# An encoder on one core: the first chunk gets an engine order of its own, its projections leave PSUM in one multiplication by the norm, and key copies, sink copies and two output weights get places at the end of a chunk

## The chip, the cores and the metric

The kernel runs on one core of one Trainium2 chip. A core has five engines that run side by side, each with its own in-order instruction queue: TensorE (PE, matrix products and transposes, results in the accumulators of PSUM), VectorE (DVE) and ScalarE (ACT) for elementwise work, GpSimd (POOL), and SyncE (SP), which here only issues DMA transfers. POOL issues some of the transfers too. Engines wait for each other through semaphores. The metric is the device time of one execution in microseconds; lower is better.

## What is computed

The reference is a two-layer encoder trunk over two independent sequences, one of 2048 and one of 512 positions, each position with 1024 channels. Layer 0 is windowed attention with grouped keys, learned sinks and a position bias; layer 1 mixes by a Fourier transform. Cut to what matters here:

```python
def attention_layer(x, g, w_in, w_out, sink, rel_bias):
    h = rmsnorm(x, g)
    z = h @ w_in                     # 16 query heads of 64, 4 key heads, 4 value heads, a gate
    q, k, v, gate = ...
    o = banded_gqa_with_sink(q, k, v, rel_bias, sink)   # keys at most 128 positions away
    return x + (o * jax.nn.silu(gate)) @ w_out

def fourier_layer(x, g, w_gate, w_out):
    h = rmsnorm(x, g)
    f = real part of the 2-D DFT of h over (positions, channels of a group), 4 groups
    return x + (f * jax.nn.silu(h @ w_gate)) @ w_out

y = rmsnorm(fourier_layer(attention_layer(x)), final_norm)   # for x_prompt and x_sample
```

In the banded attention a block of 128 queries sees the key block before it, its own and the one after it. The first and the last block of a sequence see only two. The denominator of the softmax also has the exponential of the sink.

## The kernel before

**Precision.** All products are fp32 to nearly full precision: each operand is split into a high part (a rounding copy, made by ACT) and a low part (operand minus high part, made by DVE or POOL), and a product is three matmuls: high by high, high by low, low by high (`matmul3`, line 128). A weight tile is therefore `[128, 2, 1024]`, 1 MB, made from a 512 KB fp32 tile.

**Chunks.** The attention layer runs over five chunks of 512 positions (`CHUNKS`, line 42). The first chunk, `c == 0`, is the whole short sequence; chunks 1 to 4 are the long one. In chunk 0 the weights come as fp32 (`fetch_w`, line 135, a DMA on SP), are split on the chip (`load_w`, line 144: ACT the high part, POOL the low part in four pieces), and are stored to DRAM (`wsd`, a DMA on POOL's queue). Chunks 1 to 4 load the split form from there with one DMA on SP. Split weights share four buffers (tag `w`). The fp32 tiles lie in buffers of the tags `uT` (8) and `x` (4), which other tiles use as well. Two weights of the keys (`LATE`, line 33) are split a second time in the middle of chunk 0, only to be stored; their tile takes a `w` buffer until the store has landed.

**Norms.** The norm's gain is folded into `h`. In chunks 1 to 4 the factor 1/rms is multiplied into `h` as well. In chunk 0 it isn't known early enough, so the products of `h` in raw scale are multiplied by it afterwards: `scaled` (line 366) multiplies a projection in PSUM in place (L369, DVE).

**Heads and the loop.** Eight pairs of heads `p` each need a query projection and a gate projection, in the order of the list `heads` (line 996): 16 projections, each a `Product` of 8 steps `k`, written alternately into the two PSUM banks `pj[0]` and `pj[1]`. The loop over `n` (line 1046) is a software pipeline of 19 iterations: iteration `n` works on half a pair of heads (two blocks of 128 queries) per stage of the pipeline, and PE fills the time between with the next two projections. Its order is written by hand in `PERIOD` (line 36): a list of (step, how many iterations back). Each engine's steps are chained (`seq`, line 178, and `pe`, line 184), so an engine issues them in the order of the list. Instructions that are not chained are placed by the framework's planner, which knows only their data dependences, modelled times and order in the program.

The steps, by engine:

- PE: `A` and `B` are the two projection stretches, 24 matmuls each on half the rows of the array (`beside`, line 483); in iteration `n`, `A` begins the projection `n + 2` in the bank from which projection `n` must have gone. `S1`, `S2` are the scores of two blocks (L582), `T0`, `T1` the transposes of the softmax (L641), `AV1`, `AV2` the products with the values (L682).
- DVE: `b1a` to `b2b` add bias and find the maximum (L601), `r1`, `r2` invert denominators (L615), `m1a`, `m2a`, `m2b` divide (L624, in chunk 0 L628), `lo0`, `lo1` make the low part of the transposed softmax (L658), `add` sums the values (L712), `qL` is the second operation of a projection's exit (L529 or L538).
- ACT: `e1a` to `e2b` are the exponentials (L609), `m1b` a division (L622), `hi0`, `hi1` the high parts (L654), `t2` a copy of the values (L702), `sp` the high part of the gated output (L723), `qH` the first operation of a projection's exit (L527 for a query, L536 for a gate).
- POOL: `mul` multiplies by the gate (L718), `lop` makes the low part (L727).
- `extra0`, `extra1` carry work for the next chunk or the next layer.

A projection leaves its bank through `evac_q` or `evac_g` (lines 524 and 533): in chunk 0 the multiplication L369, then ACT, then DVE, all three reading the bank.

At the head of an iteration stand, unchained, the load of the bias rows of a coming pair (`start`, line 548, a DMA on SP: `b<-rowd`) and `loads[n + 4]()` (line 1056), the weight of the projection four places on: in chunk 0 fetch, ACT's split, POOL's split and store. The sinks (`sinks`, line 560, L562) are copied into the two ends of a pair's bias tile by ACT; for the first pair of a chunk (`p == 0`) the copy is not chained.

**Between chunks.** `out_proj` (line 770) multiplies the gated outputs by the output weights in two halves of columns. The first half's products begin in the last iterations; `rest` (line 830) ends them with 48 matmuls; `evac(0)` loads the residual and adds it; then `mm(1, k)` runs the second half, 96 matmuls, and asks for a weight tile (`load(1, m)`) at every second `k`. For all but the last chunk these steps run at the beginning of the next chunk, together with `make_h` (line 249: DMA `xk`, POOL L263, ACT L267, DVE L268) and `kv_proj` (line 374), which makes keys and values and copies the last 256 key columns of the chunk before to the front (L381, DVE, not chained).

After the five chunks `fourier_phase` (line 1088) does layer 1; the change does not touch it.

Of the kernel before, what the change touches and what calls it, by code (L numbers as in the profile page):

```python
# [40 lines left out]
)  # L41
# [8 lines left out]
def encoder(  # L50
# [93 lines left out]
    def load_w(c, n, name, lo_engine=None, late=None, w32=None):  # L144

        w = wp.tile([P, 2, D], F32R, align_bytes=LINE, tag="w", bufs=4, name=f"w{name}")
        if c == 1 and n in AGAIN:
            w32 = xtile([P, D], F32, f"w32{name}")
            SP.dma_start(w32, w_in[n])
            ACT.copy(w[:, 0], w32)  # L150
            DVE.tensor_tensor(w[:, 1], w32, f32(w[:, 0]), ALU.subtract)
            POOL.dma_start(f32(wsd[n]), f32(w))
            return w[:, 0], w[:, 1]
        if c:
            SP.dma_start(f32(w), f32(wsd[n]))
            return w[:, 0], w[:, 1]
        if w32 is None:
            w32 = fetch_w(n, name, late)
        ACT.copy(w[:, 0], w32)
# [27 lines left out]
    def attention_phase():  # L187

        with ExitStack() as es:
# [184 lines left out]
            def kv_proj(c, hs, halo, norms=None, early=None):  # L374
# [4 lines left out]
                if not first:  # L379
                    for g in range(4):  # L380
                        DVE.tensor_copy(kwin[g][:, :, 0:256], f32(kwin[g][:, :, 512:768]))  # L381
# [125 lines left out]
            def qg_proj(c, which, p, place, hs, res, invb=None):  # L507

                n = 12 + p if which == "g" else p
                st = {}  # L510

                def fetch():
                    st["w32"] = fetch_w(n, f"{which}{c}_{p}")
# [8 lines left out]
                out = Product(place, left, lambda k: hs[k])  # L522

                def evac_q():
                    ps = scaled(out.ps, invb, f"q{p}")
                    qab = ap.tile([P, 2, CH], F32R, align_bytes=LINE, tag="qab", bufs=2, name=f"qab{c}_{p}")
                    seq(ACT, ACT.activation(qab[:, 0], ps, AF.Copy, scale=-0.125))  # L527
                    res["q"] = qab
                    return lambda: seq(DVE, DVE.scalar_tensor_tensor(  # L529
                        qab[:, 1], ps, -0.125, f32(qab[:, 0]), ALU.mult, ALU.subtract  # L530
                    ))

                def evac_g():
                    ps = scaled(out.ps, invb, f"g{p}")
                    th = ap.tile([P, CH], F32, tag="tmp", bufs=2, name=f"th{c}_{p}")
                    seq(ACT, ACT.activation(th, ps, AF.Tanh, scale=0.5))  # L536
                    s = res["s"] = ap.tile([P, CH], F32, tag="s", bufs=2, name=f"s{c}_{p}")
                    return lambda: seq(DVE, DVE.scalar_tensor_tensor(s, th, 1.0, ps, ALU.add, ALU.mult))  # L538

                return fetch, load, out, evac_g if which == "g" else evac_q  # L540

            def attention(c, p, res, uTs):
# [17 lines left out]
                def sinks():  # L560

                    ends = ACT.copy(  # L562
                        st["bias"][:, :, 0:386:385], sk[:, 2 * p : 2 * p + 2, None].to_broadcast([P, 2, 2])
                    )
# [205 lines left out]
            def out_proj(c, uTs):  # L770
# [5 lines left out]

                def product(half, i):
# [63 lines left out]
                return load, outs[0], steps  # L841
# [138 lines left out]
            for c in range(len(CHUNKS)):  # L980
# [16 lines left out]
                fetches, loads, o, evacs = zip(*(  # L997
                    qg_proj(c, which, p, pj[i % 2], hs, res[p], invb0) for i, (which, p) in enumerate(heads)
                ))
                load_op, op_tiles, op = out_proj(c, uTs)  # L1000
# [9 lines left out]
                evacs[0]()()  # L1010
# [34 lines left out]
                low_q = []  # L1045
                for n in range(19):
# [1101 lines left out]
```

## Time and profile before

| what | us |
|---|---|
| three runs | 1593.91, 1595.08, 1597.87 (median 1595.08) |
| the profiled execution | 1601.03 |
| its span, first to last instruction | 1599.2 |
| loop of chunk 0 (39.3 to 205.3 us of the span) | 166.0, PE busy 150.7, DVE 111.5, ACT 112.0, POOL 82.7 |
| boundary to chunk 1, then its loop | 70.7 (PE busy 70.6), 144.0 (142.1) |
| the same of chunk 2 | 68.0 (67.4), 146.0 (144.1) |
| the same of chunk 3 | 67.5 (66.9), 145.5 (144.0) |
| the same of chunk 4 | 65.0 (61.6), 142.0 (141.0) |
| the Fourier layer | 545.2 (534.9) |

The mean granted TensorE clock is 0.993 of full speed; in the loop of chunk 0 it is 0.97, in the boundary to chunk 4 0.95. A row of a timeline reads: start, duration, engine, line, operation, output and input tiles, shape, count, and in brackets how long the engine was idle before and what ended that. A row of the waits reads: who waited for whom, us in total, times, longest. A row of the chain: start, duration, what. A row of a table by stage: from and to, length, then PE, weight loads, DVE, ACT and POOL busy with their instruction counts in parentheses, clock, DMA share, GB/s.

### The profile page before, as it was taken

Reading aid. Unit: us, or ns where it says so; the run is one execution under the profiler, and the core shown is the slowest. Engines: PE = TensorE matmul, PEld = TensorE weight load, DVE = VectorE, ACT = ScalarE, POOL = GpSimd, SP = SyncE. Lnnn points to the kernel's source line nnn. Section 1 sums busy time; section 2 is a strip of 40 time slices with the busy share of each in tenths; the row PEclk is TensorE's granted clock in tenths of the full one; section 3 lists DMA queues with packets and bytes.
Section 4 is the critical chain, followed back from the end, with each engine's and each line's share of the span. In section 5 each row is a group of like instructions: output and inputs, shape, how many; then the busy total and the mean of one; then the engine's idle time right before and its main releaser. Section 6 shows DMA issues by size and latency. Waiting matters only on the chain.

```text
span 1599.2 us, 33480 instructions
## 1 busy us (share of the span) xinstructions
PE 1559.9 (98%) x12977; PEld 1362.8 (85%) x12977; DVE 1135.7 (71%) x2503; ACT 892.3 (56%) x1960; POOL 448.9 (28%) x614
## 2 busy tenths in 40 slices
PE   9899899999999999999999999999999999999998
PEld 7788788999898888888887899988888888888886
DVE  6667636777626876447773277758898898989886
ACT  7677624677516786247872277755565664233342
POOL 3455463432411513304214143123121211111100
PEclk9999999999999999999999999999999999999999
DMA  8566588676676664856747666574766569656852
GB/s 330 222 240 227 178 301 287 214 247 228 222 282 207 218 240 149 329 201 207 275 142 284 238 231 221 219 281 151 261 209 213 195 232 385 242 186 233 308 195 92
DMA packets 100442, 372.70 MB, mean 233 GB/s; under 512 B 11203, under 2 KB 22219, under 8 KB 82876
## 3 DMA queue, kind: packets, MB, share of 16 engines
q1 hardware_dynamic: 82716, 297.38, 53.2%
q0 software_dynamic: 16400, 70.04, 11.2%
q10 hardware_dynamic: 1168, 3.15, 0.6%
q8 instruction: 102, 1.67, 0.4%
q14 instruction: 56, 0.46, 0.1%
HBM read 280.06 MB, written 90.47 MB: 232 GB/s over the span
## 4 chain that ended last, share of the span: by engine, by line
PE 78%; DVE 8%; DMA 6%; ACT 4%; issue 3%; POOL 1%; POOLq 0%; ACTq 0%; SPq 0%; DVEq 0%
PE pj L493 25%; PE av L682 5%; PE W L131 5%; PE spt L582 5%; PE tp L131 5%; PE pj L131 5%; PE av L131 4%; PE tp L641 3%; PE spt L131 3%; PE Wo L131 3%; PE Z L131 2%; PE fo L131 2%; PE z L1261 2%; DMA wo<-wsd 2%; PE Zo L131 2%
## 5 line engine op out<-in xcount | busy, mean ns | idle before, releaser
L493 PE MATMUL pj<-h,wg 64*128 64x512 f32 x1920 | 445.7, 392 | 1.8 <-DVE s L538 1.4
L493 PE MATMUL pj<-h,wq 64*128 64x512 f32 x1560 | 382.5, 390 | 6.1 <-DVE qab L529 6.1
L493 PEld LDWEIGHTS pj<-h,wg 64*128 64x128 f32 x1920 | 332.3, 185 | 25.7 <-DVE s L538 3.3
L493 PEld LDWEIGHTS pj<-h,wq 64*128 64x128 f32 x1560 | 285.2, 185 | 30.3 <-DVE qab L529 8.9
L601 DVE CUSTOM_DVE_ANT_0 S<-spt,b 128x385 f32<-128x385 f32 (+1 forms) x320 | 167.2, 524 | 103.7 <-PE spt L582 101.7
L609 ACT ACTIVATE S<-S 128x385 f32<-128x385 f32 (+1 forms) x320 | 189.7, 593 | 82.5 <-DVE S L601 57.7
L654 ACT CAST pts<-tp 128x768 fp32r<-128x768 f32 (+1 forms) x160 | 121.3, 758 | 89.8 <-PE av L682 53.1
L658 DVE TENSOR_TENSOR pts<-tp,pts 128x768 fp32r<-128x768 f32 (+1 forms) x160 | 143.9, 899 | 20.2 <-ACT pts L654 19.8
L682 PE MATMUL av<-pts,v 64*128 64x256 f32 x1680 | 144.9, 288 | 7.0 <-ACT pts L654 3.5
L682 PEld LDWEIGHTS av<-pts,v 64*128 64x128 f32 x1680 | 127.8, 186 | 12.4 <-DVE pts L658 4.9
L727 POOL TENSOR_TENSOR uT<-o,uT 128x256 fp32r<-128x256 f32 x75 | 56.3, 750 | 251.9 <-ACT uT L723 251.7
L582 PE MATMUL spt<-kwin,qab 64*128 64x384 f32 (+1 forms) x960 | 123.2, 339 | 1.7 <-ACT qab L527 1.3
L131 PE MATMUL fo<-wo,tTu 128*128 128x512 f32 x480 | 115.1, 392 | 0.0
L131 PEld LDWEIGHTS fo<-wo,tTu 128*128 128x128 f32 x480 | 88.3, 188 | 17.3
L641 PEld LDWEIGHTS tp<-ident,S 64*128 64x128 f32 x1792 | 93.8, 138 | 10.2 <-DVE pts L658 3.9
L641 PE MATMUL tp<-ident,S 64*128 64x64 f32 x1792 | 97.1, 224 | 0.8 <-DVE pts L658 0.7
L582 PEld LDWEIGHTS spt<-kwin,qab 64*128 64x128 f32 x960 | 86.5, 187 | 4.6 <-ACT qab L527 1.7
L624 DVE TENSOR_SCALAR S<-S 128x384 f32<-128x384 f32 (+1 forms) x192 | 89.0, 492 | 0.1
L493 PE MATMUL pj<-wo,uT 64*128 64x512 f32 x360 | 77.9, 399 | 5.4 <-DVE s L538 5.4
L718 POOL TENSOR_TENSOR o<-o,s 128x256 f32<-128x256 f32 x75 | 55.7, 743 | 92.1 <-DVE o L712 67.0
L131 PE MATMUL tp<-wo,uT 128*128 128x512 f32 x240 | 63.2, 400 | 4.5 <-DMA wo<-wsd 4.5
L493 PEld LDWEIGHTS pj<-wo,uT 64*128 64x128 f32 x360 | 57.6, 189 | 10.5 <-DVE s L538 6.8
(365 smaller groups left out, 3356.9 us busy)
## 6 DMA issues: line engine op xcount, KB each, us to landing
wo<-wsd SPq DMA_DIRECT2D x32, 1024.0 KB, 6.7
wq<-wsd SPq DMA_DIRECT2D x31, 1024.0 KB, 6.5
wg<-wsd SPq DMA_DIRECT2D x31, 1024.0 KB, 6.0
x<-x1d SPq DMA_DIRECT2D x40, 512.0 KB, 3.8
b<-b21d SPq DMA_DIRECT2D x40, 512.0 KB, 6.5
b<-rowd SPq DMA_DIRECT2D x40, 384.0 KB, 4.1
xs<-in_x_dram SPq DMA_DIRECT2D x23, 512.0 KB, 6.2
s2d<-gt POOLq DMA_DIRECT2D x40, 256.0 KB, 3.9
```

The source lines that it names most:

```text
L131: ins = pe(PE.matmul(out, a[i], b[j], start=start and i + j == 0, stop=stop and i == 1, skip_group_check=more))
L493: out.last[h] = pe(PE.matmul(out.ps, a[i], b[j], **out.flags()))
L582: pe(PE.matmul(spt[j][:, 2 + k0 * P : 2 + k1 * P], res["q"][rows, qp, b * P : (b + 1) * P], kwin[g][rows, kp, b * P + k0 * P : b * P + k1 ...
L601: seq(DVE, DVE.tensor_tensor_reduce(out=s[:, e0:e1], in0=ps[:, 1 + e0 : 1 + e1], in1=st["bias"][:, j, 386 - e1 : 386 - e0][:, ::-1], scale ...
L609: last_exp[0] = seq(ACT, ACT.activation(s[:, e0:e1], s[:, e0:e1], AF.Exp, bias=s[:, 386:387], scale=-1.0, accum_out=s[:, 387:388]))
L624: seq(DVE, DVE.tensor_scalar(s[:, ks], s[:, ks], den, None, ALU.mult))
L641: pe(PE.transpose(ps[h][:, kb, j, :], s[rows, j, 1 + kb * P : 1 + (kb + 1) * P], ident[rows, rows]))
L654: seq(ACT, ACT.copy(hi, ps))
L658: seq(DVE, DVE.tensor_tensor(lo, ps, f32(hi), ALU.subtract))
L682: last[i][h] = pe(PE.matmul(av[:, i, :256], v[rows], pt[rows], start=not swap and n == 0, stop=swap and n == len(todo[h]) - 1, skip_group_ ...
L718: eng.tensor_tensor(o, o, s, ALU.mult)
L727: low = eng.tensor_tensor(lo, o, f32(hi), ALU.subtract)
```

## The change

Chunk 0 gets the order `FIRST`; the others keep `PERIOD`. In `FIRST` the exit of a projection has one step more: `sc` (DVE) multiplies the bank by the norm into an SBUF tile, `qH` and `qL` work on that tile. The weight of a coming projection is only fetched at the head of an iteration; ACT's split is the step `W`, POOL's split and the store are the step `WL` of the next iteration (`split_w`). Key copies are chained on DVE, the sinks of a chunk's first pair on ACT (but for chunk 0). In `rest` two weight tiles of the second half are asked for ahead of the residuals (but for chunk 0).

```diff
+FIRST = (
+    ("AV1", 2), ("sc", 1), ("extra0", 0), ("extra1", 0), ("lop", 3), ("T0", 1), ("AV2", 2), ("r2", 1), ("m2a", 1), ("WL", 0),
+    ("S1", 0), ("t2", 2), ("m2b", 1), ("A", 0), ("hi0", 1), ("b1b", 0), ("qH", 1), ("b1a", 0), ("lo0", 1), ("e1b", 0),
+    ("e1a", 0), ("qL", 1), ("T1", 1), ("r1", 0), ("add", 2), ("S2", 0), ("hi1", 1), ("mul", 2), ("B", 0), ("b2a", 0),
+    ("m1b", 0), ("W", 0), ("b2b", 0), ("lo1", 1), ("e2a", 0), ("m1a", 0), ("e2b", 0), ("sp", 2),
+)
...
+    def split_w(c, n, name, w32):
+        w = wp.tile([P, 2, D], F32R, align_bytes=LINE, tag="w", bufs=4, name=f"w{name}")
+        seq(ACT, ACT.copy(w[:, 0], w32))
+        def low():
+            for i in range(4):
+                cs = slice(i * 256, i * 256 + 256)
+                POOL.tensor_tensor(w[:, 1, cs], w32[:, cs], f32(w[:, 0, cs]), ALU.subtract)
+            if n not in LATE + AGAIN:
+                POOL.dma_start(f32(wsd[n]), f32(w))
+        return (w[:, 0], w[:, 1]), low
...
-                        DVE.tensor_copy(kwin[g][:, :, 0:256], f32(kwin[g][:, :, 512:768]))
+                        seq(DVE, DVE.tensor_copy(kwin[g][:, :, 0:256], f32(kwin[g][:, :, 512:768])))
...
+                def normed_q():
+                    whole = ap.tile([P, CH], F32, tag="tmp", bufs=2, name=f"q{c}_{p}")
+                    place(DVE.scalar_tensor_tensor(whole, out.ps, -0.125, invb[:, :CH], ALU.mult, ALU.mult))
+                    def high():
+                        qab = pair_of()
+                        seq(ACT, ACT.copy(qab[:, 0], whole))
+                        return lambda: seq(DVE, DVE.tensor_tensor(qab[:, 1], whole, f32(qab[:, 0]), ALU.subtract))
+                    return high
+                def normed_g():
+                    s = res["s"] = ap.tile([P, CH], F32, tag="s", bufs=2, name=f"s{c}_{p}")
+                    place(DVE.tensor_tensor(s, out.ps, invb[:, :CH], ALU.mult))
+                    def high():
+                        th = ap.tile([P, CH], F32, tag="tmp", bufs=2, name=f"th{c}_{p}")
+                        seq(ACT, ACT.activation(th, s, AF.Tanh, scale=0.5))
+                        return lambda: seq(DVE, DVE.scalar_tensor_tensor(s, th, 1.0, s, ALU.add, ALU.mult))
+                    return high
...
-                    if p:
+                    if p or c:
                         seq(ACT, ends)
-                    elif not c:
+                    else:
                         after(ends, last_inv[0])
...
-                    if half and k % 2 == 0:
+                    if half and k % 2 == 0 and (half, k // 2) not in st:
                         load(half, k // 2)
...
                 def rest():
                     for k in range(6):
                         outs[0][0].whole(k)
+                    if c:
+                        load(1, 0)
+                        load(1, 1)
                     for k in (4, 5):
                         outs[0][1].whole(k)
...
                     if n < 16:
-                        loads[n + 4]()
+                        (loads if c else fetches)[n + 4]()
                     chain.setdefault(PE, None)
                     first, second = fills(n)
-                    for name, back in PERIOD:
+                    for name, back in PERIOD if c else FIRST:
                         m = n - back
...
                         elif name == "qH":
+                            if c and 0 <= m < 15:
+                                high_q.append(evacs[m + 1])
+                            if high_q:
+                                low_q.append(high_q.pop()())
+                        elif name == "sc":
                             if 0 <= m < 15:
-                                low_q.append(evacs[m + 1]())
+                                high_q.append(evacs[m + 1]())
+                        elif name == "W":
+                            if n < 16:
+                                low_w.append(highs[n + 4]())
+                        elif name == "WL":
+                            if low_w:
+                                low_w.pop()()
```

More of the change, by code (lines that the diff above doesn't have):

```diff
@@ L505, in swapped, with qg_proj @@
                         tc.add_manual_dep(wait.ins, ins.ins.name, DONE, reason="other rows of a bank")
-            def qg_proj(c, which, p, place, hs, res, invb=None):
+            def qg_proj(c, which, p, bank, hs, res, invb=None):
                 n = 12 + p if which == "g" else p
@@ L520, in left, with pair_of @@
                     return [t[:, ks] for t in st["w"]]
-                out = Product(place, left, lambda k: hs[k])
+                out = Product(bank, left, lambda k: hs[k])
+                def pair_of():
+                    qab = ap.tile([P, 2, CH], F32R, align_bytes=LINE, tag="qab", bufs=2, name=f"qab{c}_{p}")
+                    res["q"] = qab
+                    return qab
                 def evac_q():
[L525 to L528, printed above, removed]
+                    st["qab"] = qab = pair_of()
+                    seq(ACT, ACT.activation(qab[:, 0], out.ps, AF.Copy, scale=-0.125))
@@ L542, in attention, with place @@
+                def place(ins):
+                    if PE in chain:
+                        seq(DVE, ins)
+                if invb is None:
+                    evac = evac_g if which == "g" else evac_q
+                else:
+                    evac = normed_g if which == "g" else normed_q
+                return fetch, high, load, out, evac
             def attention(c, p, res, uTs):
@@ L1009, in attention_phase @@
                     o[0].whole(k)
-                evacs[0]()()
+                step = evacs[0]
+                while callable(step):
+                    step = step()
                 loads[2]()
```

30 lines of the change are left out of this document (20 added, 10 removed).

## The prediction

> **What bounds the kernel now.** I read the page's busy shares, then the waits of PE, the chain of waits by time, and the timelines of DVE, ACT, PE and SP where the chain gets longer.
>
> ```profile
> PE 1559.9 (98%) x12977; PEld 1362.8 (85%) x12977; DVE 1135.7 (71%) x2503; ACT 892.3 (56%) x1960; POOL 448.9 (28%) x614
> ```
> ```profile
> PE pj L493 <- DVE s L538: 6.8, 7, 2.8
> PE pj L493 <- DVE qab L529: 6.6, 11, 1.5
> PE tp L131 <- DMA wo<-wsd: 4.5, 3, 3.4
> ```
> ```profile
> 130.24 2.85 PE pj L493 x23
> ...
> 149.25 2.86 PE pj L493 x23
> ...
> 309.06 2.80 PE pj L493 x24
> ...
> 326.35 2.80 PE pj L493 x24
> ```
> ```profile
> 46.45 0.70 DVE L369 TENSOR_TENSOR pj<-pj,invb 128x512 f32<-128x512 f32 x1 [0.26 <-PE pj L493]
> 55.57 0.70 DVE L369 TENSOR_TENSOR pj<-pj,invb 128x512 f32<-128x512 f32 x1 [0.34 <-PE pj L493]
> ...
> 188.66 0.70 DVE L369 TENSOR_TENSOR pj<-pj,invb 128x512 f32<-128x512 f32 x1 [0.36 <-PE pj L493]
> ```
>
> PE is the bound, so only PE's waits and slow stretches are worth anything. The first wait lines name the projection bank `pj` and who frees it. In the chain, two iterations of the first chunk take 149.25 - 130.24 = 19.01 us, two of the next chunk 326.35 - 309.06 = 17.29 us, though the first chunk's attention is the narrower (two of its four blocks see two key blocks instead of three, against one of four). The norm multiplication of L369 happens once per iteration n = 1 to 15: 188.66 - 46.45 = 142.2 us for 14 intervals, 9.1 for the first and 133.1 for the other 13, 10.2 each. Why is shown by one iteration:
>
> ```profile
> 117.99 0.70 DVE L369 TENSOR_TENSOR pj<-pj,invb 128x512 f32<-128x512 f32 x1 [0.34 <-PE pj L493]
> 119.43 0.58 ACT L536 ACTIVATE th<-pj 128x512 f32<-128x512 f32 x1
> 120.04 0.69 DVE L538 SCALAR_TENSOR_TENSOR s<-th,pj 128x512 f32<-128x512 f32 x1 [1.36 <-ACT th L536]
> 120.78 0.50 PE L493 MATMUL pj<-h,wg 64*128 64x512 f32 x1 [0.50 <-DVE s L538]
> 129.03 0.39 PE L493 MATMUL pj<-h,wg 64*128 64x512 f32 x1
> ```
>
> The bank is multiplied at 117.99, read by ACT at 119.43 and by DVE until 120.73; only then does stretch "A" run on (120.78). In the next iteration A's first matmul stands at 129.03, its partner for the other bank would follow about 0.1 us later. So an iteration in which the bank is free takes about 129.1 - 120.75 = **8.4 us** of PE work.
>
> **The change, part by part.**
>
> *Bank freed by one multiplication.* `sc` multiplies out of PSUM into SBUF; ACT and the second DVE operation then read SBUF. The count of operations stays: one multiplication, one ACT copy or tanh, one DVE operation. Prices of the SBUF forms, which this stage did not have:
>
> ```profile
> L906 ACT CAST e<-w32e x24: 605/610/624, 307.6 to 979.4; 128x512 fp32r<-128x512 f32 x24
> ```
> ```profile
> L1111 DVE TENSOR_TENSOR S<-s,S x40: 677/682/742, 1096.3 to 1314.6; 128x512 fp32r<-128x512 f32 x40
> ```
>
> 0.61 and 0.68 us, the same as 0.58 and 0.69 above: zero. The bank is free 0.34 + 0.70 = 1.04 us after the last matmul of B instead of about 3.1. Between B and A, PE has the values, the transposes and the first scores, which end just before 129.03, 1.5 us after B's last matmul (127.5, from the same rows: 0.34 us before the multiplication, one interval later). The wait should be gone, with 0.5 us to spare.
>
> *What is late next.* By engine work the stage still fits:
>
> ```profile
> 120.00:140.00 20.00, 18.19 (x204) 16.39 (x204) 15.02 (x46) 16.17 (x39) 10.67 (x17) 1.00 0.61 228
> ```
>
> DVE 15.02 and ACT 16.17 us in 20, that is 7.1 and 7.6 us per 9.46 us iteration, against 8.4. Fitting the new order to these durations by hand, ending `lo1` (which the values of the next iteration need) leaves DVE some 0.5 us. One thing eats into it: the low part of a projection now has two SBUF inputs while POOL subtracts weights (`WL`), where before one input was in PSUM. L1111 above, with two SBUF inputs, shows 0.68 us where nothing is in the way; L268 has two as well, and runs here while POOL multiplies `xk`:
>
> ```profile
> 858.47 1.43 DVE L268 SCALAR_TENSOR_TENSOR h<-xk,g0s,h 128x512 fp32r<-128x512 f32 x1 [0.24 <-ACT h L267]
> ```
>
> So the low part costs 0 to 0.75 us more; I take 0.4 for it and every other misfit, nearest to the middle of the two rows: 8.8 us per interval. [...]
>
> *Weight split, moved.* `W` (ACT, about 1.05 us) moves from just ahead of the projection's ACT step to behind `m1b`; the four POOL pieces (`WL`) and the 1 MB store's issue on POOL move behind `lop` of the next iteration. Queued behind `W` are `e2a`, `e2b` and `sp`; DVE's `m2a`, `m2b` wait for these, then PE's transposes. SP's fetch stays at the iteration's head, so it has more time than before. The two late weights (L159) are what the old order waited for:
>
> ```profile
> 73.22 1.05 ACT L159 CAST wq<-w32q 128x1024 fp32r<-128x1024 f32 x1 [3.28 <-DMA wsd<-wlate]
> ...
> 94.97 1.04 ACT L159 CAST wq<-w32q 128x1024 fp32r<-128x1024 f32 x1 [4.00 <-DMA wsd<-wlate]
> ```
>
> The copy sat in ACT's queue until the late tile's store had landed. In the new order it comes some 6 us later in the iteration and can take the buffer that B frees. Bounds: all 7.3 us stay, or none; I take 1 us for each, nearer to none, because the 6 us are more than either wait. First chunk then: 13 x 8.8 = 114.4, plus the first interval without its wait for `qab` (9.1 - 1.5 by the longest wait above) 7.6, plus 2: 124.0 against 142.2, **18.2 us** less.
>
> *Sinks.* The copy of the sinks for the next chunk's first head (L562) had no place and slid into ACT's queue ahead of work of the current loop:
>
> ```profile
> 176.91 0.20 ACT L562 COPY b<-sk 128x4 f32<-128x4 f32 x1 [3.19 <-DMA b<-rowd]
> 395.45 0.20 ACT L562 COPY b<-sk 128x4 f32<-128x4 f32 x1 [2.09 <-DMA b<-rowd]
> 608.75 0.20 ACT L562 COPY b<-sk 128x4 f32<-128x4 f32 x1 [2.24 <-DMA b<-rowd]
> 821.82 0.20 ACT L562 COPY b<-sk 128x4 f32<-128x4 f32 x1 [1.87 <-DMA b<-rowd]
> ```
> ```profile
> 384.82 0.60 ACT L527 ACTIVATE qab<-pj 128x512 fp32r<-128x512 f32 x1 [0.39 <-PE pj L493]
> ...
> 403.69 0.60 ACT L536 ACTIVATE th<-pj 128x512 f32<-128x512 f32 x1 [0.54 <-PE pj L493]
> ```
>
> The first is in the 142.2 us already. Around the second, two iterations take 403.69 - 384.82 = 18.87 instead of 17.29 us: 1.58 lost for a wait of 2.09, three quarters. For the last three waits, 6.2 us in all, that is **4.7 us**; bounds 3.1 (half) and 6.2. Behind the last operation of the loop the DMA has long landed: no new wait.
>
> *Key copies.* Twelve on DVE, 0.42 us each, pass from the middle of a loop to its end. PE hardly waited for DVE there, so nothing is gained; at the end DVE does 1.7 us three times ahead of work that PE needs much later (its 144 output matmuls lie between). Zero; at most 5 lost.
>
> ```profile
> L381 DVE CAST kwin<-kwin x12: 414/418/425, 297.8 to 829.3; 128x512 fp32r<-128x512 f32 x12
> ```
>
> *Output weights ahead.* In the last boundary between chunks:
>
> ```profile
> 851.01 2.32 SPq L261 DMA_DIRECT2D xk<-in_xT_dram  x4
> ```
> ```profile
> 853.42 7.93 DMA wo<-wsd
> 861.39 2.93 PE tp L131 x6
> ...
> 868.65 1.36 PE av L131 x6
> ```
>
> The load of `wo` stood behind four loads of `xk` in SP's queue, which waited for DVE. PE stood still until 861.39 and then ran three groups of six in 868.65 - 861.39 = 7.26 us instead of 3 x 1.36: 3.2 us more. With the 4.5 us of all three boundaries: 7.7. Now two of the loads are issued once `rest` has used up their buffers (12 matmuls, about 2.7 us in), ahead of residuals and `xk`; landing 7.9 us later they come just in time for the 48 matmuls of `rest` (10.9 us at 1.36 per six). What they push back, `xk`, is delayed by some 3 us and feeds the next chunk's projections after another 96 matmuls. **7.7 us**; bounds 4.5 and 7.7.
>
> Sum: 18.2 + 4.7 + 7.7 = 30.6 us. The profiled execution took 1601.0 us with a span of 1599.2; its span would be 1568.6. The median of the runs shown is 1595.08, 6 us lower than the profiled one; the waits are in both, so I subtract there: **1564.5 us**.
>
> **The rivals.**
>
> *DVE and POOL in each other's way become the bound.* With 0.75 us in each interval: 13 x 9.15 + 7.6 + 2 = 128.6, 13.6 saved, 26.0 in all: 1569.1. For it: DVE's margin is some 0.5 us. Against: POOL's 10.67 us in 20 leave half the time without a meeting.
>
> *The first chunk's order does not do what it says*: PE gets the bank earlier and waits as long for transposes or values; only the sinks' 3.19 us go there. 3.2 + 4.7 + 7.7 = 15.6: 1579.5.
>
> *Slower: `W` waits in every iteration.* Place: ACT's queue, ahead of `e2a`; cause: no free weight buffer until B has ended, or a fetch that is not there. ACT is free 19% of the time, about 1.7 us per iteration. What exceeds that is PE's loss, 16 times. Break-even is a wait of 1.7 + 30.6 / 16 = 3.6 us each time; at the 4.00 us seen above, 16 x 2.3 = 36.8 is lost, 6.2 more than gained: 1601.3. Against: four buffers hold the three weights in use and one free.
>
> **How the numbers follow.** Forecast 0.60, DVE against POOL 0.22, no gain from the order 0.08, `W` waits in every iteration 0.10, half of it near break-even and half beyond. About 0.3% (4.8 us) is what a measurement of this kernel can tell from no change. Faster 0.90, within it 0.05, slower 0.05. The bounds: most, 13 x 8.4 + 7.6 = 116.8, so 25.4 + 6.2 + 7.7 = 39.3: 1556; least, 13 x 9.15 + 7.6 + 7.3 = 133.9, so 8.3 + 3.1 + 4.5 = 15.9: 1579. With the second rival's 1579.5 the range is 1556 to 1581.
>
> **What would show it.** Right: no wait of `pj` for DVE in the first chunk and intervals of 8.4 to 9 us between its norm multiplications; no wait of L562 for `rowd` in the loops; SP issuing `wo` ahead of `xk` and no wait of PE for `wo`. Wrong: PE waiting for `pts` or `S` of DVE in the first chunk (first rival), L159's group with long waits there (third), or a wait for the residuals or `xk` at the boundaries.

## The result, and the profile after

| | before | after |
|---|---|---|
| median of the runs, us | 1596.34 (1593.91 to 1597.87, 4 runs) | 1580.13 (1579.22 to 1580.90, 4 runs) |
| the profiled execution, its span, us | 1601.03, 1599.2 | 1580.90, 1579.1 |
| mean granted TensorE clock | 0.993 | 0.995 |

The ratio is 0.99, with a 95% interval of 0.9882 to 0.9917: the change makes the kernel 16 us, 1%, faster. The forecast was 1564.5 in a range of 1556 to 1581. Sign and range held, the range by its last microsecond; half of the forecast gain of 30.6 us did not come.

The table by stage shows where. Chunk 0 is cut at the first and the last multiplication of `pj` by the norm (DVE), which gives 14 intervals; the other chunks are cut at the first and the last query that leaves `pj`. A boundary to chunk 2, 3 or 4 therefore still holds the last two iterations of the loop before it, and with them the sinks' wait. Columns: stretch, length, then PE, weight loads, DVE, ACT and POOL busy with counts, granted clock, DMA share, GB/s. First the kernel before:

```profile
46.45:188.66 142.21, 127.92 (x1386) 114.98 (x1383) 97.70 (x308) 99.32 (x228) 73.47 (x106) 0.96 0.60 220
188.66:273.04 84.38, 83.46 (x548) 72.52 (x546) 45.81 (x85) 36.21 (x71) 44.16 (x56) 1.00 0.77 272
...
385.45:483.41 97.96, 95.88 (x732) 85.08 (x729) 50.66 (x112) 38.09 (x90) 27.76 (x31) 1.00 0.66 237
598.49:696.87 98.38, 96.17 (x750) 85.63 (x747) 51.50 (x113) 38.83 (x90) 27.73 (x31) 1.00 0.66 236
811.93:909.44 97.51, 92.85 (x698) 81.75 (x695) 42.37 (x96) 33.39 (x72) 27.88 (x34) 0.96 0.67 243
```

The same stretches after:

```profile
46.82:181.22 134.40, 125.46 (x1387) 115.16 (x1383) 100.89 (x307) 95.94 (x227) 73.61 (x105) 0.95 0.67 233
181.22:265.19 83.97, 82.98 (x549) 72.29 (x546) 44.98 (x85) 36.02 (x72) 46.27 (x60) 1.00 0.83 291
...
377.61:473.62 96.01, 95.43 (x732) 85.41 (x729) 51.44 (x116) 38.00 (x90) 27.73 (x31) 1.00 0.67 242
588.68:685.69 97.01, 95.96 (x750) 84.71 (x747) 52.21 (x115) 38.80 (x90) 28.01 (x31) 1.00 0.66 239
800.76:890.84 90.08, 89.38 (x698) 78.82 (x695) 44.51 (x100) 33.39 (x72) 27.52 (x34) 1.00 0.70 263
```

Chunk 0's loop lost 7.8 us of the 18.2 forecast. Everything else lost 20.1 - 7.8 = 12.3 us, as much as the 12.4 forecast for sinks and output weights, most of it (7.4) in the boundary to chunk 4. In chunk 0 PE is still idle for 8.9 us of 134.4, and its clock is 0.95. The longest of PE's waits, whole run, after:

```profile
PE tp L698 <- DVE pts L715: 9.3, 6, 3.8
```

The old leaders are gone from its head: the bank `pj` released by DVE's second operation, and `wo`. New on top are the transposes (`tp`), the step `T1` waiting for the low part of the softmax (`lo0`). The two longest of these waits:

```profile
62.92 0.90 PE L698 MATMUL tp<-ident,S 64*128 64x64 f32 x12 [3.79 <-DVE pts L715]
85.92 0.90 PE L698 MATMUL tp<-ident,S 64*128 64x64 f32 x12 [3.01 <-DVE pts L715]
```

What they do to the loop, the DVE timeline says: the multiplications out of the bank, one per iteration (L569 a query, L580 a gate).

```profile
46.82 0.69 DVE L569 SCALAR_TENSOR_TENSOR q<-pj,invb 128x512 f32<-128x512 f32 x1 [1.32 <-PE pj L513]
54.31 0.69 DVE L580 TENSOR_TENSOR s<-pj,invb 128x512 f32<-128x512 f32 x1 [0.60 <-PE pj L513]
69.56 0.69 DVE L569 SCALAR_TENSOR_TENSOR q<-pj,invb 128x512 f32<-128x512 f32 x1 [2.33 <-PE pj L513]
78.10 0.69 DVE L580 TENSOR_TENSOR s<-pj,invb 128x512 f32<-128x512 f32 x1
91.39 0.69 DVE L569 SCALAR_TENSOR_TENSOR q<-pj,invb 128x512 f32<-128x512 f32 x1 [1.16 <-PE pj L513]
103.54 0.69 DVE L580 TENSOR_TENSOR s<-pj,invb 128x512 f32<-128x512 f32 x1 [1.25 <-PE pj L513]
112.09 0.69 DVE L569 SCALAR_TENSOR_TENSOR q<-pj,invb 128x512 f32<-128x512 f32 x1 [0.45 <-PE pj L513]
```

The first interval is 7.49 us, an undisturbed one 8.54 or 8.55. (A later one of 10.23 us, 10.16 in the old order, is in all the kernels here.) Three are long: 15.25, 13.29 and 12.15. What ACT does in them (the weight copies of its timeline):

```profile
59.88 1.04 ACT L165 CAST wlate<-w32late 128x1024 fp32r<-128x1024 f32 x1 [5.46 <-DMA w32late<-in_w_in_dram]
68.69 1.05 ACT L180 CAST wg<-w32g 128x1024 fp32r<-128x1024 f32 x1 [3.62 <-issue]
...
82.88 1.04 ACT L165 CAST wlate<-w32late 128x1024 fp32r<-128x1024 f32 x1 [4.36 <-DMA w32late<-in_w_in_dram]
92.99 1.05 ACT L180 CAST wg<-w32g 128x1024 fp32r<-128x1024 f32 x1 [4.91 <-issue]
```

Each LATE weight makes ACT wait twice: its own copy (L165) stands in ACT's queue until its fetch has landed, and the next `W` (L180) stands until the late tile has given its buffer back. For this second wait the rows name no releaser ("issue"). That it is the buffer is read from the store: issued at 64.54 and 87.53 us, the second landed after 5.4 us, at 92.93, just ahead of the `W` at 92.99, and the last packets of the first moved at about 68.4, just ahead of the `W` at 68.69. The run with tiles of its own, below, has no such wait. The old order had the second wait (3.28 and 4.00 us) but not the first:

```profile
64.68 1.05 ACT L159 CAST wlate<-w32late 128x1024 fp32r<-128x1024 f32 x1 [0.58 <-issue]
...
85.72 1.05 ACT L159 CAST wlate<-w32late 128x1024 fp32r<-128x1024 f32 x1 [0.54 <-PE pj L493]
```

The late copy is chained in neither kernel. It is called in the step `extra1`, which carries more than work for the next chunk, and `FIRST` has this step in the fourth place where `PERIOD` has it in the eighteenth. In the old order the copy ran 64.68 - 54.27 = 10.4 us after its fetch had been issued; in the new one its turn comes at 59.88 - 5.46 = 54.42, 1.5 us after (SP's rows, before and after):

```profile
54.27 0.46 SPq L138 DMA_DIRECT2D w32late<-in_w_in_dram  x1
```
```profile
52.95 0.46 SPq L144 DMA_DIRECT2D w32late<-in_w_in_dram  x1
```

No run moves `extra1` alone. So the theory for the experiments is that **the two LATE weights take about 15 us of chunk 0, where 2 were allowed**.

### The profile page after: what moved, and what is told of

Its sections match the earlier page's. It is cut to its first block, busy times and chain, and to the rows that moved or that the text cites. A ratio compares the mean times of both kernels' runs of the same rounds, so it can differ in the third digit from the quotient of the medians.

```text
span 1579.1 us, 33455 instructions
## 1 busy us (share of the span) xinstructions
PE 1552.4 (98%) x12977; PEld 1359.2 (86%) x12977; DVE 1139.7 (72%) x2503; ACT 888.4 (56%) x1960; POOL 449.0 (28%) x614
## 3 DMA queue, kind: packets, MB, share of 16 engines
q8 instruction: 102, 1.67, 0.4%
## 4 chain that ended last, share of the span: by engine, by line
PE 84%; DVE 5%; DMA 4%; issue 3%; ACT 2%; POOL 1%; SPq 0%; POOLq 0%; DVEq 0%; ACTq 0%
PE pj L513 26%; PE av L739 6%; PE W L137 5%; PE pj L137 5%; PE spt L639 5%; PE fo L137 5%; PE tp L137 4%; PE av L137 4%; PE tp L698 4%; PE Wo L137 3%; PE spt L137 3%; PE Z L137 3%; PE Zo L137 2%; PE z L1343 2%; PE ABp L137 1%
## 5 line engine op out<-in xcount | busy, mean ns | idle before, releaser
L639 PE MATMUL spt<-kwin,qab 64*128 64x384 f32 (+1 forms) x960 | 122.0, 341 | 1.4 <-ACT qab L573 1.2
L513 PE MATMUL pj<-wo,uT 64*128 64x512 f32 x360 | 74.5, 390 | 0.0
L769 DVE TENSOR_TENSOR o<-av,t 64x256 f32<-64x256 f32 x150 | 61.9, 413 | 1.6 <-ACT t L759 0.5
L759 ACT COPY t<-av 64x512 f32<-64x512 f32 x80 | 46.7, 584 | 28.0 <-PE av L747 16.4
```

The costliest lines, as they stand in the source:

```text
L513: out.last[h] = pe(PE.matmul(out.ps, a[i], b[j], **out.flags()))
L639: pe(PE.matmul(spt[j][:, 2 + k0 * P : 2 + k1 * P], res["q"][rows, qp, b * P : (b + 1) * P], kwin[g][rows, kp, b * P + k0 * P : b * P + k1 ...
L769: seq(DVE, DVE.tensor_tensor(o[64 * j : 64 * j + 64], ps[0:64, :, j], t2[:, :, j], ALU.add))
```

## Experiments on the LATE weights

Intervals are read as above; "loop" is the 14 intervals of chunk 0, "boundary 1" the stretch to chunk 1's first query (134.40 and 83.97 in the changed kernel). Every time has the kernel before beside it on the same chip, 1598.97 us in this group.

**Without the late split.** Chunk 1 splits the two weights instead.

```diff
-        if c == 1 and n in AGAIN:
+        if c == 1 and n in AGAIN + LATE:
...
-                    if c == 0 and i % 8 == 3 and 1 <= i // 8 < 3:
-                        load_w(0, LATE[i // 8 - 1], f"late{i // 8}", late=last_exp[0])
```

> The two LATE weights are taken out of chunk 0's loop altogether; their split is done again at the start of chunk 1, as the AGAIN weights' is already, so no part of the result is left out. Theory (the two LATE weights cost the loop of chunk 0 about 15 us in the changed kernel, where the prediction allowed 2): the 14 intervals of chunk 0 shrink from 134.4 us to 119-121 (13 of 8.55 and the first of 7.5, about 118.7, and the 0.6 of the one at 10.23), the three long ones (15.25, 13.29, 12.15) become 8.6, and the whole run comes to 1565-1568 us, with 0 to 2 us given back where chunk 1 splits the two weights itself. Rival (the shortfall lies in the new order itself: the W copies wait in ACT's queue, LATE or not): the intervals stay near 130 us in all and the run within 3 us of the changed kernel, 1577-1581. Rival (the ends of the chunks gave less than forecast): the loop as the theory says or not, but the rest of the span falls behind by several us; the stages outside chunk 0 tell.

Measured: 1576.75 us, ratio 0.9857 (0.9839 to 0.9875).

```profile
48.34:167.76 119.42, 119.08 (x1387) 112.56 (x1382) 99.63 (x307) 93.65 (x225) 65.36 (x93) 1.00 0.67 231
167.76:262.41 94.65, 87.14 (x549) 74.87 (x546) 49.19 (x87) 38.19 (x74) 47.36 (x62) 0.95 0.78 286
```

The loop falls by 15.0 us to 119.42, with PE busy for 119.08 of it and the clock at 1.00: as the theory said, and the three long intervals are 8.56, 8.57 and 8.54. Of the 15.0 us, 8.6 were idle time of PE (8.94 against 0.34) and 6.4 were PE running slower (busy 125.46 against 119.08 for the same 1387 matmuls, at a clock of 0.95 against 1.00). The cost of splitting them in chunk 1 was misjudged: 10.7 us come back in boundary 1, not 0 to 2, which is why the whole run gained so little.

**Fetched earlier.** Only the wait for the transfer should go.

```diff
+                    if c == 0 and i in (6, 14):
+                        late_w.append(fetch_w(LATE[i // 8], f"late{i // 8}", last_exp[0]))
                     if c == 0 and i % 8 == 3 and 1 <= i // 8 < 3:
-                        load_w(0, LATE[i // 8 - 1], f"late{i // 8}", late=last_exp[0])
+                        load_w(0, LATE[i // 8 - 1], f"late{i // 8}", late=last_exp[0], w32=late_w.pop(0))
```

> The fetches of the two LATE weights are issued about half an iteration to one and a half earlier than their split, so that the late copy no longer waits in ACT's queue for its own transfer (5.46 and 4.36 us in the changed kernel); its buffer is still one of the four of the split weights. Theory (both waits cost): the two waits for the transfer go, the two of the W copies for a buffer (3.62 and 4.91 us) stay; 5 to 9 us of the 15 come back, the run 1571-1575. Rival (the transfer alone costs, the wait for the buffer is a consequence of it): 12 to 15 us come back, 1565-1568. Rival (the buffer alone costs, it ends later anyway): 0 to 2 us, 1578-1580.

Measured: 1575.07 us, ratio 0.9847 (0.9831 to 0.9863); loop 129.15, 5.3 us less.

```profile
53.81 1.05 ACT L165 CAST wlate<-w32late 128x1024 fp32r<-128x1024 f32 x1
67.51 1.04 ACT L180 CAST wg<-w32g 128x1024 fp32r<-128x1024 f32 x1 [7.08 <-DMA wsd<-wlate]
...
78.98 1.05 ACT L165 CAST wlate<-w32late 128x1024 fp32r<-128x1024 f32 x1 [1.79 <-PE pj L513]
88.57 1.05 ACT L180 CAST wg<-w32g 128x1024 fp32r<-128x1024 f32 x1 [3.16 <-issue]
```

No late copy waits for its transfer any more, but the first `W` now waits 7.08 us for the late store instead of 3.62: part of one wait had been hiding the other.

**Tiles of its own.** Only the wait for the buffer should go.

```diff
+    def split_late(n, name, w32):
+        hi, lo = xtile([P, D], F32R, f"hi{name}"), xtile([P, D], F32R, f"lo{name}")
+        ACT.copy(hi, w32)
+        for i in range(4):
+            cs = slice(i * 256, i * 256 + 256)
+            POOL.tensor_tensor(lo[:, cs], w32[:, cs], f32(hi[:, cs]), ALU.subtract)
+        POOL.dma_start(f32(wsd[n][:, 0]), f32(hi))
+        POOL.dma_start(f32(wsd[n][:, 1]), f32(lo))
...
-                        load_w(0, LATE[i // 8 - 1], f"late{i // 8}", late=last_exp[0])
+                        nm = f"late{i // 8}"
+                        split_late(LATE[i // 8 - 1], nm, fetch_w(LATE[i // 8 - 1], nm, last_exp[0]))
```

> The high and low parts of a LATE weight go to two tiles of another pool (each 4 KB a partition) and are stored by two transfers, so that the W copies of the loop have all four buffers of the split weights to themselves; the fetch is issued as late as in the changed kernel. Theory (both waits cost): the waits of the W copies for a buffer (3.62 and 4.91 us) go, those of the late copies for their transfer (5.46 and 4.36 us) stay; 4 to 7 us of the 15 come back, the run 1573-1576. Rival (the transfer alone costs): 0 to 3 us, 1577-1580. Rival (the buffer alone costs): 12 to 15 us, 1565-1568.

Measured: 1571.98 us, ratio 0.9841 (0.9817 to 0.9864); loop 124.30, 10.1 us less.

```profile
58.35 1.05 ACT L193 CAST hilate<-w32late 128x1024 fp32r<-128x1024 f32 x1 [3.88 <-DMA w32late<-in_w_in_dram]
63.13 1.04 ACT L180 CAST wg<-w32g 128x1024 fp32r<-128x1024 f32 x1
...
77.88 1.05 ACT L193 CAST hilate<-w32late 128x1024 fp32r<-128x1024 f32 x1 [3.52 <-DMA w32late<-in_w_in_dram]
```

No `W` waits any more, and more came back than the 4 to 7 us expected. That doesn't make the buffer the larger part: the waits for the transfers are shorter here too (3.88 and 3.52 us for 5.46 and 4.36), and the clock stays at 1.00, so that 5.9 of the 10.1 us are PE's busy time (119.57 for 125.46). In the changed kernel the two longest gaps of PE, 3.79 and 3.01 us, stand behind the late copies, and one of 1.81 behind a `W`. How the 15.0 us divide between the two waits is not shown. What remains here are the two waits for transfers, and two intervals of 11.01 and 10.97.

**Both.** The two edits together.

> Both edits together: the LATE weights are fetched earlier and split into tiles of their own. Theory: neither wait is left, the late split costs ACT 2 x 1.04 us and POOL 2 x 4 instructions beside the rest; 11 to 15 us of the 15 come back, the run 1565-1569, within 3 us of the kernel with the LATE weights taken out of the loop. Rival (what costs is the half clock or the order of the chain, set off by any foreign instruction in ACT's queue): no more than the better of the two single edits.

Measured: **1566.12 us, ratio 0.9796 (0.9779 to 0.9813)**, better than both kernels; the changed kernel's interval begins at 0.9882.

```profile
46.63:167.75 121.12, 119.51 (x1387) 111.88 (x1383) 102.44 (x307) 94.77 (x227) 73.75 (x107) 1.00 0.72 254
```

13.3 of the 15.0 us are back and boundary 1 is 84.3, as in the changed kernel. The late split as such costs 121.12 - 119.42 = 1.7 us; the waits it caused in ACT's queue cost the other 13.3. The two single edits gave 5.3 and 10.1: both theories of a single cause fall. Their sum of 15.4 is more than the 13.3 of both together, so the two don't simply add.

**The same in the old order.** The first of these edits, made to the kernel before.

> The kernel before, with the two LATE weights out of the loop of chunk 0 and split again in chunk 1, the same edit as was made to the changed kernel: there it took 15.0 us off the 14 intervals of chunk 0 (134.40 to 119.42) and gave 10.7 us back between chunk 0 and chunk 1 (83.97 to 94.65). Theory (the LATE weights cost the old order about half as much, and the new one made their cost grow): the 14 intervals go from 142.2 to 134-136 us, 6 to 8 us less, 10 to 11 us come back behind it, the run is 2 to 5 us longer than before, ratio 1.001 to 1.004. Rival (they cost the old order as much, and the new order only failed to remove it): the intervals go to 127-129 us, the run is 3 to 5 us shorter, ratio 0.997.

Measured: 1599.97 us against 1597.91 for before, ratio 1.002 (1.0005 to 1.0034). The loop goes from 142.21 to 135.14, boundary 1 from 84.38 to 95.19. The old order paid 7.1 us for the LATE weights, close to its two waits (7.3); the new order pays 15.0. Without LATE weights the two orders stand at 135.14 and 119.42. The last interval of the old one, 14.84 us, contains the sinks; at 9.09, as it is without them (next section), the comparison is 129.4 to 119.4. **The order is worth 10 us without the LATE weights, and 8 of them go back through these.** "The order" is here the list with the exit from the bank and the moved weight split that belong to it; no run takes these apart.

## Experiments on the ends

The kernel before took 1597.91 us beside the ends alone, the kernel without early output weights and the one with the old sinks, and 1598.94 beside the others. "Boundaries" are the stretches to chunks 2, 3 and 4: before 97.96, 98.38, 97.51; after 96.01, 97.01, 90.08.

**The ends alone.** The kernel before with sinks, key copies and early output weights as in the change, chunk 0 as it was.

> The ends alone: the kernel before, with the sinks and the key copies in the chains and the two output weights ahead of the residuals; chunk 0 keeps PERIOD, its projections' exits and its weight split of before. Theory (the ends gave what was forecast, 12.4 us, and the loop of chunk 0 fell short): the stages after chunk 0 are as in the changed kernel, 12 us shorter than before; in chunk 0 only the sinks' wait of 3.19 us goes, worth 0 to 3 us; the ratio to before is 0.990 to 0.9925. Rival (the ends alone give less, because part of the 12 us came from the order of chunk 0): ratio above 0.994. Rival (the new order of chunk 0 gave nothing of its own, the 7.8 us there are the sinks' wait): the loop of chunk 0 is as short as in the changed kernel, 134 us, ratio 0.988.

Measured: 1583.08 us, ratio 0.9915 (0.9898 to 0.9932), inside the theory's 0.990 to 0.9925. Boundaries 96.19, 96.62, 90.03, as in the changed kernel. In chunk 0 the loop is 136.49, 5.7 less than before: the last interval goes from 14.49 to 9.09, more than the 0 to 3 us expected. In the old order the sinks' wait of 3.19 us ended in a PE wait of 2.85 us and a stretch at half clock (0.50 from 179 to 183 us), 5.4 us in all. So the ends account for most of the measured gain: the new order takes chunk 0's loop only from 136.49 to 134.40, and in the times its 2 us are not shown, as the intervals of the two kernels overlap.

**Without the early output weights.**

```diff
-                    if c:
-                        load(1, 0)
-                        load(1, 1)
```

> The changed kernel without the two early loads of output weights in the run-out of the first half. Forecast of the term: 7.7 us (4.5 to 7.7), all of it in front of chunk 4, where the loads of residuals and xk are ahead of the output weights in SP's queue. Theory: the stretch from the last query of chunk 3 to the first of chunk 4 goes from 90.1 back to 96-97.5 us, the waits of PE for wo come back (3 to 4.5 us), the run is 4.5 to 8 us longer than the changed kernel. Rival (the early loads gave nothing, the 7.4 us there come from the sinks or the key copies): under 2 us longer.

Measured: 1580.31 us, ratio 0.9898 (0.9881 to 0.9915): no difference from the changed kernel. Boundary to chunk 4: 91.43, only 1.35 more, where 96 to 97.5 was expected. The forecast of the term falls in this form. SP's queue shows why:

```profile
836.89 0.37 SPq L161 DMA_DIRECT2D wo<-wsd  x1
838.91 2.37 SPq L281 DMA_DIRECT2D xk<-in_xT_dram  x4
841.38 3.29 SPq L161 DMA_DIRECT2D wo<-wsd  x3
```

Without being asked to, the planner now puts one load of `wo` ahead of `xk`, and PE's longest wait for it is 0.4 us. Which of the other edits moved it was not separated.

**The early output weights alone**, in the kernel before.

> The kernel before with the two early loads of output weights and nothing else of the change. By the forecast: 7.7 us less than before, all in front of chunk 4 (97.5 to 89.8). Theory: PE's waits for wo go (2.9 to 4.5 us), the stretch falls to 90-91.5 us, and the median of the times by 2 to 4 us (ratio 0.9975 to 0.9985), since the half clock was not in most executions. Rival (the early loads are worth nothing even by themselves, as in the changed kernel without them, whose times were the same): the median within 1 us of before.

Measured: 1593.49 us, ratio 0.9965 (0.9951 to 0.998), 5.6 us, more than the 2 to 4 expected; the boundary to chunk 4 is 91.18. By itself the edit does what the prediction said of it, though the middle value is below 7.7: the next runs show a reason.

**The kernel before, profiled twice more.**

> The kernel before itself, unchanged, for a second profiled execution. The first one took 1601.0 us, 5 to 6 more than the median, and in front of chunk 4 PE waited 3.39 us for an output weight that took 7.93 us to land, and then ran at half its clock; the kernel before with only its LATE weights changed waited 1.67 us there (landing about 6.2) and kept its clock. Theory (that wait is partly an accident of the one profiled execution): the stretch from the last query of chunk 3 to the first of chunk 4 is 93 to 95 us, not 97.5, with no half clock, and the span is 1594 to 1597. Rival (the wait belongs to the kernel): 97 to 98 us again. The rest of the stretches as in the first profile within 0.7 us: 142.2, 84.4, 98.0, 98.4.

> The same once more, for a third profiled execution: the same two expectations for the stretch in front of chunk 4, 93 to 95 us or 97 to 98.

Measured: 1596.45 and 1601.49 us; the boundary to chunk 4 is 95.57 and 95.37. PE's rows there, from the profile before, the two repeats, and the kernel before without the late split:

```profile
861.39 2.93 PE L131 MATMUL tp<-wo,uT 128*128 128x512 f32 x6 [3.39 <-DMA wo<-wsd]
864.12 2.76 PE L131 MATMUL av<-wo,uT 128*128 128x512 f32 x6
```
```profile
859.29 2.66 PE L131 MATMUL tp<-wo,uT 128*128 128x512 f32 x6 [2.71 <-DMA wo<-wsd]
861.75 2.15 PE L131 MATMUL av<-wo,uT 128*128 128x512 f32 x6
```
```profile
863.20 2.73 PE L131 MATMUL tp<-wo,uT 128*128 128x512 f32 x6 [2.48 <-DMA wo<-wsd]
865.73 2.08 PE L131 MATMUL av<-wo,uT 128*128 128x512 f32 x6
```
```profile
863.59 1.66 PE L131 MATMUL tp<-wo,uT 128*128 128x512 f32 x6 [1.67 <-DMA wo<-wsd]
865.08 1.52 PE L131 MATMUL av<-wo,uT 128*128 128x512 f32 x6
```

Both boundaries lie between the two expectations. The wait belongs to the kernel, but its size doesn't: 3.39, 2.71, 2.48 and 1.67 us, with a slow stretch behind the first three (granted clock 0.55 from 864 to 868 us, 0.62 from 860 to 864 and 0.64 from 864 to 868; a group of six takes 1.52 at full clock), shorter in the repeats, and none behind the last (1.00 from 864 to 868). My expectation of no half clock was wrong. The profile that the prediction was worked out from was 2 us unluckier here than either repeat. The rest of a profile varies as well: the loop of chunk 0 took 142.21, 141.05 and 143.69.

**Sinks as before**, in the changed kernel.

```diff
-                    if p or c:
+                    if p:
...
-                    else:
+                    elif not c:
```

> The changed kernel with the sinks' copy for a chunk's first pair put back out of ACT's chain (as before). Forecast of the term: 4.7 us (3.1 to 6.2) in the loops of chunks 1 to 3, and 3.2 us of waiting in the loop of chunk 0 that were counted there. Theory: the stretches from the last query of one chunk to the first of the next, 96.0, 97.0 and 90.1 us, get 1.4 to 2 us longer each, the loop of chunk 0 0 to 4 us longer; in all 4 to 9 us over the changed kernel. Rival (chained key copies, not the sinks, gave the 2 and 1.4 us of the first two boundaries): no change there.

Measured: 1582.91 us, ratio 0.9916 (0.9898 to 0.9935). Boundaries 96.81, 98.22, 91.04: 0.80 + 1.21 + 0.96 = 3.0 us more, less than the 1.4 to 2 us each that were expected. (Cut at the last gate instead of the last query, the loops of chunks 1 to 3 are 1.48 + 1.57 + 1.14 = 4.2 us longer, near the forecast 4.7; the stretches behind them come out about 1.2 us shorter.) In chunk 0's loop the copy waits 1.98 us, and the last interval is 8.65 against 8.63: the new order hides it there.

**Key copies as before**, in the changed kernel.

> The changed kernel with the key copies out of DVE's chain again, placed by the planner as before. Forecast of the term: zero, at most 5 us. Theory: the two stretches in front of chunks 2 and 3 (96.0, 97.0) grow by 0 to 1 us each, the run is within 2 us of the changed kernel. Rival (the copies in the middle of the loop were what delayed the ends): 3 to 6 us longer, some of it inside the loops of chunks 2 to 4 (115.1 us each from first to last query) or in SP's order of the output weights.

Measured: 1579.70 us, ratio 0.9884 (0.9863 to 0.9906); boundaries 96.37, 97.15, 89.90. Nothing, as forecast.

## Why the prediction was right, and where it was not

The sign, the bound and the mechanism of the main term were right. That the time lies in the range is in part luck: its upper end comes from the second rival, by which the order does nothing, and the forecast's own least gain ended at 1579. Step by step:

- **Bank freed by one multiplication: right.** PE's waits for `pj` in chunk 0 shrink to 0.3 us, and an undisturbed interval takes 8.55 us, between the floor of 8.4 and the 8.8 taken. The first interval is 7.49 for 7.6.
- **DVE and POOL in each other's way: avoided, not borne.** In the steady intervals the low part of a query takes 0.68 us: the weight split `WL`, which the prediction saw as the other party, never runs beside it. Twice in chunk 0 it takes twice as long, in iterations that a LATE weight had upset, and there it meets POOL's `lop`:

```profile
73.55 1.31 DVE L574 TENSOR_TENSOR qab<-q,qab 128x512 fp32r<-128x512 f32 x1
...
97.84 1.28 DVE L574 TENSOR_TENSOR qab<-q,qab 128x512 fp32r<-128x512 f32 x1
```
```profile
73.55 0.75 POOL L784 TENSOR_TENSOR uT<-o,uT 128x256 fp32r<-128x256 f32 x1
...
97.83 0.74 POOL L784 TENSOR_TENSOR uT<-o,uT 128x256 fp32r<-128x256 f32 x1
```

  The two low parts took 0.63 and 0.60 us longer there than the 0.68 of a steady interval. What such a meeting would cost in every interval, no run here shows. Of the 0.4 per interval for it and every other misfit, 8.55 - 8.4 = 0.15 was needed; the rest was too much, 2.6 us over the loop (122.0 without the LATE term, measured 119.4).
- **The LATE weights: the step that failed.** The prediction said that `W` "comes some 6 us later in the iteration and can take the buffer that B frees", and took 1 us for each of two weights. Measured: 15.0, against bounds of 0 to 7.3. `W` still waited (3.62 and 4.91 us); and the late copy itself, whose place the prediction does not mention, came to another one in ACT's queue with the step `extra1`, where it waits for its own transfer (5.46 and 4.36 us). That wait, and the lower clock behind PE's three gaps (0.50, 0.59 and 0.69 over the 4 us behind each; 6.4 of the 15.0 us), had no place in the term, so the upper bound was too low as well. The waits reach PE through what is queued behind the copies on ACT (`t2`, `hi0`) and DVE's `lo0`, which waits 4.87 and 4.09 us for `hi0` and for which the transposes wait (3.79 and 3.01 us).
- **Sinks: right in kind, somewhat too large.** 3.0 us in the last three boundaries for 4.7, just under the lower bound of 3.1; in the loops alone 4.2. In chunk 0 of the old order they had cost 5.4, where the rival's sum had 3.2.
- **Key copies: right**, zero.
- **Output weights: right mechanism, size not confirmed.** Alone 5.6 us for 7.7, which the interval (3.2 to 7.8) only just holds; inside the change 1.4, where a load comes forward without being asked for.
- **From one profile to the median: wrong.** "The waits are in both, so I subtract there." The profile pair differs by 20.1 us, the medians by 16.2. The profiled execution before was 5 us above its median, and 2 us of that lay in the very wait that was counted in full.

The sum: against the profile the gain was forecast 30.6 - 20.1 = 10.5 us too high, of which +13.0 is the LATE term and -2.6 the interval; the ends agree within 0.1, their parts offsetting. The remaining 5 us are the profile's distance from the median (3.9) and a median of before that came out 1.3 higher. With the LATE waits taken away, the kernel is at 1566.12, 33 us below its kernel before (1598.97) where the forecast had 30.6. So the forecast is near for an order that leaves the two weights out of ACT's way, and the changed kernel isn't that; that the time itself lies only 1.6 us from the forecast is luck, as errors of both signs meet in it.

The slower rival, `W` waiting in every iteration, met two iterations of 16, with waits of 3.62 and 4.91 us; PE's gap of 1.81 us stands behind the second, none behind the first, and after the three long intervals no `W` waits. That the order does nothing (1579.5) comes nearest to the measured time, for another reason: the order gave 10 us and lost 8, and the sinks in chunk 0 gave 5.4.

The same LATE waits cost 15.0 us in the profile of the changed kernel and 12 to 14 in the three kernels without early output weights, with the old sinks and with the old key copies (loops of 133.13, 131.63 and 132.81). The difference lies in PE's busy time, 125.46 us against 123.05, 123.55 and 123.11 at clocks of 0.95 and 0.97, not in its idle time (8.9 against 10.1, 8.1 and 9.7).

What stays open: which edit moved the first `wo` load ahead of `xk`, how the 15.0 us divide between transfer and buffer, and what decides whether a gap of PE is followed by a lower clock (0.50 to 0.69 behind the three gaps of the changed kernel).

## What to carry to other kernels

When an order is written out by hand, list every instruction of the stage that is *not* in it, and what a step like `extra1` carries along: each can be placed anew, as the late copy was here, which held ACT's queue for 5.46 and 4.36 us until its transfer was there, and behind it a `W` for 3.62 and 4.91 us until its buffer was. Fetch early and give side work buffers of its own before packing a loop tightly: the same two weights cost 7.1 us in the old order, where ACT waited for them twice, and 15.0 in the new, where it waited four times. And before a wait from a single profile is subtracted from a median, ask what in it is the landing time of one transfer in one execution: PE's wait for `wo` was 3.39, 2.71 and 2.48 us in three profiles of the same kernel.

## Not expected of the hardware

The granted TensorE clock was lower behind some short gaps of PE and not behind longer ones: 0.69 over the 4 us behind a gap of 1.81 us, 1.00 behind one of 2.44. PE's row behind the changed kernel's third long gap, and the stretch of 4 us from there in the table by stage:

```profile
97.98 0.59 PE L698 MATMUL tp<-ident,S 64*128 64x64 f32 x12 [1.81 <-DVE pts L715]
```
```profile
98.00:102.00 4.00, 4.00 (x36) 3.35 (x38) 3.96 (x10) 3.66 (x10) 2.47 (x4) 0.69 0.65 268
```

The same of the kernel without early output weights:

```profile
61.49 0.59 PE L698 MATMUL tp<-ident,S 64*128 64x64 f32 x12 [2.44 <-DVE pts L715]
```
```profile
62.00:66.00 4.00, 4.00 (x49) 3.49 (x46) 3.92 (x12) 1.33 (x4) 2.12 (x3) 1.00 0.55 233
```

So the clock fell behind the gap of 1.81 us and not behind the one of 2.44. Above, it did not fall behind 1.67 us either (1.00 from 864 to 868 us), but did behind 2.71 and 2.48 us (0.62 from 860 to 864 us, 0.64 from 864 to 868). The length of a gap by itself doesn't decide; what else does, these runs don't show.
